# A two-layer fp32 mixer: a third plain feature tile, weight sums on VectorE, and layer 1's modulation moved into the down passes

## The chip, the cores and the metric

The kernel runs on one core of a Trainium2 chip. The metric is the device time of one execution in microseconds (us). Engines: PE (TensorE, matmuls), DVE (VectorE), ACT (ScalarE), POOL (GpSimd) and SP (SyncE), which issues all DMA transfers of this kernel.

## What is computed

Two layers of a transformer-like mixer on 512 latent tokens (stream X) and 256 context tokens (stream C), width 1024. The change touches the second half of a layer and the modulation vectors:

```python
for l in range(2):
    mod = silu(c) @ w_mod[l] + b_mod[l]          # 6 vectors of 1024; the same for c_ctx
    ...                                          # attention, local mixers -> mix
    x = layer_norm(ALPHA * x + g1 * (mix @ w_out), ln1g, ln1b)
    h = x * (1.0 + sc2) + sh2
    ffn = (silu(h @ w1) * (h @ w3)) @ w2         # 1024 -> 2816 -> 1024
    x = layer_norm(ALPHA * x + g2 * ffn, ln2g, ln2b)
```

Layer 0 does this for both streams (768 tokens), layer 1 for X alone (512).

## The kernel before

All matrix products are in fp32 made of three matmuls: `split` (L167 to L169) makes of an operand a high part (an ACT cast, L168) and a low part (a DVE subtraction, L169), and `mm3` (L172 to L174) adds low x high, high x low and high x high. Tokens lie in two halves of N columns, N = 384 in layer 0 and 256 in layer 1.

**The up phase** is `wout_ffn`. After the output projection and the first layer norm, `half` transposes a half's tokens and splits them into R[0] or R[1]. The 2816 hidden features are 22 tiles of 128. The first NCONV = 2 are plain: `conv` multiplies a tile's two weights (w1, w3) with one half, 48 matmuls, so 96 a tile. The other 20 are block tiles: seven products of 12 matmuls (`prod`, L1186) with sums of weights of N columns, 84 a tile. `up_forms` makes the sums: splits wa (of s1, for a11 and a12), wb (for s1 and a22), wc (for s2 and s4) and wd (for s3), with four 128x512 sums on POOL between them (L1073, L1074, L1077, L1078); wc hangs on all but one. The token side needs the differences T1 to T4 of the halves (L1177 to L1180), three kinds on DVE, one on POOL, and their splits. T3 takes over the buffers of R[1][0:4]. After the products, ACT copies partial sums (L1232 is one), DVE adds (L1194, L1218, L1233), and POOL multiplies by the gate (L1195, L1196). The output of a tile goes to DRAM (`yd`).

`spool` also writes the residual of the second layer norm to DRAM (`rd`): `residual` (L964) scales and shifts it first, two 128x1024 POOL operations (L966, L967) a token tile.

**The down phase** runs in passes: layer 0 in two passes of three token tiles, layer 1 in one of four. For each feature tile, `feat` loads its `yd` columns and its w2 weight, splits them, and `mm` multiplies; one feature tile is loaded ahead. At ft == 6 the residual comes back. `ffn_last` is the second layer norm (L1021 to L1046). After tiles X1 and X2 of pass 1, `hook` makes layer 1's first operands (groups of transposes, L360).

**Modulation of layer 1.** `mods` loads 512 KB pieces of w_mod, two for each of eight k groups, and multiplies them in small matmuls (L274), four a group. Three such generators are in `filler`; `fill(2)` takes two steps after each block tile of layer 0.

**What sets the order.** The order of the instructions on each engine is set by a scheduler that simulates the program; buffers come from pools in which a new tile waits for an old one's last reader (weights w 5, raw weights s 4, u 22, f 14 in the FFN, PSUM pairs pd 2, PSUM banks ps 4). Each engine, SP too, runs its own list in order.

Of the kernel before, what the change touches and what calls it, by code (L numbers as in the profile page):

```python
# [90 lines left out]
def hybrid_kernel(ctx: ExitStack, tc: tile.TileContext, out: bass.AP, g: dict):  # L91
# [996 lines left out]
    def wout_ffn(l, streams, final, hook=None):  # L1088
# [100 lines left out]
        def finish(ft, w, A, Bk, sa, su):  # L1189

            prod(A, w["s4"], B22, False, True)
            A_.activation(out=sa[:, 1], in_=A, func=AF.Silu)  # L1192
            prod(Bk, w["a22"], T4, False, True)
            V_.tensor_tensor(out=su[:, 0], in0=su[:, 0], in1=Bk, op=ALU.add)  # L1194
            G_.tensor_tensor(out=sa[:, 1], in0=sa[:, 1], in1=su[:, 1], op=ALU.mult)  # L1195
            G_.tensor_tensor(out=sa[:, 0], in0=sa[:, 0], in1=su[:, 0], op=ALU.mult)  # L1196

        def store(ft, sa):
            nc.sync.dma_start(out=yd[l][ft][:, :2 * N], in_=sa.rearrange("p a b -> p (a b)"))

        wn = up_forms(l, NCONV)
# [302 lines left out]
```

## Time and profile before

| | us |
|---|---|
| median of 3 runs (1714.37 to 1716.43) | 1716.4 |
| the profiled execution | 1715.44 |
| its span, first to last instruction | 1713.7 |
| PE busy in the span | 1590.8 (93%) |
| DVE busy | 1009.1 (59%) |
| ACT busy | 771.0 (45%) |
| POOL busy | 613.7 (36%) |

The mean granted clock of PE is 0.977 of full speed. Stages of the span, in us: layer 0's plain tiles end at 468, its block stage runs from 489 to some 850, its down passes to 1033; the boundary to layer 1 takes till 1080; layer 1's plain tiles run from 1314 to 1342, its block stage from 1350 to some 1580, its down pass from 1599 to 1703.

A busy share is a mean over stages with different limits; what an edit is worth is read in its own stage, from the idle time before an instruction (in brackets in a timeline row, with what ended it) and from what the releasing engine did meanwhile. In a timeline row the first number is the start, the second the time from the first start to the last end of xcount instructions; the step from one row's start to the next is what they cost.

### The profile page before, as it was taken

What the parts mean: (1) busy time and instruction counts of PE and PEld (TensorE: products, weight loads), DVE (VectorE), ACT (ScalarE), POOL (GpSimd) and SP (SyncE); (2) the same over time, 40 slices, a digit from 0 to 9 for tenths busy, and PEclk for the clock granted to TensorE, in tenths of its full rate; (3) what the DMA queues carried; (4) which work ended last, traced back from release to release, by engine and by line L of the source; (5) the groups of instructions that cost most, each with busy time, mean ns of one, the idle gap of its engine ahead of it and who ended that gap; (6) DMA issues with size and microseconds to landing.
All of it is one profiled execution on the core that took longest, in us unless ns stands there. A gap on an engine that the chain in (4) does not pass through costs nothing.

```text
span 1713.7 us, 24043 instructions
## 1 busy us (share of the span) xinstructions
PE 1590.8 (93%) x9105; PEld 1363.9 (80%) x9105; DVE 1009.1 (59%) x1361; ACT 771.0 (45%) x1381; POOL 613.7 (36%) x570
## 2 busy tenths in 40 slices
PE   6999889999859999999899998989999799997997
PEld 4757779887848777799888887879988798996886
DVE  1434777869853343354455437677769766567645
ACT  2422666865332232333443336478844444453311
POOL 0213012325635444455200105523325577772002
PEclk9999999999979999999999998999999899998999
DMA  9575113145335656634774625401164333456521
GB/s 336 169 230 169 58 38 118 56 147 185 108 119 179 198 168 182 187 127 122 228 228 130 207 70 168 125 25 38 38 221 144 109 116 114 123 161 193 174 86 50
DMA packets 180216, 241.81 MB, mean 141 GB/s; under 512 B 10842, under 2 KB 126924, under 8 KB 180100
## 3 DMA queue, kind: packets, MB, share of 16 engines
q1 hardware_dynamic: 180100, 240.28, 44.2%
q8 instruction: 71, 1.16, 0.3%
q14 instruction: 45, 0.37, 0.1%
HBM read 215.30 MB, written 24.94 MB: 140 GB/s over the span
## 4 chain that ended last, share of the span: by engine, by line
PE 69%; DVE 13%; DMA 5%; ACT 5%; issue 4%; POOL 3%; SPq 1%; DVEq 0%; POOLq 0%; ACTq 0%
PE pd L1186 18%; PE pd L172 9%; PE pd L173 9%; PE pd L174 9%; PE ps L274 4%; PE ps L172 4%; DVE u L169 4%; PE ps L174 4%; PE ps L173 4%; DVE w L169 3%; PE ps L731 3%; PE ps L1186 3%; PE ps L715 2%; ACT w L168 2%; DMA s<-in_w_ffn_dram 2%
## 5 line engine op out<-in xcount | busy, mean ns | idle before, releaser
L169 DVE TENSOR_TENSOR w<-s,w 128x1024 fp32r<-128x1024 f32 (+2 forms) x287 | 391.5, 1371 | 283.9 <-ACT w L168 282.0
L168 ACT CAST w<-s 128x1024 fp32r<-128x1024 f32 (+2 forms) x287 | 293.8, 1030 | 477.0 <-PE pd L1186 116.7
L1186 PE MATMUL pd<-u,w 128*128 128x256 f32 (+1 forms) x2040 | 320.6, 310 | 46.7 <-DVE w L169 30.3
L1186 PEld LDWEIGHTS pd<-u,w 128*128 128x128 f32 x2040 | 296.8, 191 | 76.6 <-DVE w L169 31.1
L172 PE MATMUL pd<-w,u 128*128 128x512 f32 (+5 forms) x728 | 276.2, 380 | 12.3 <-DVE u L169 6.4
L173 PE MATMUL pd<-w,u 128*128 128x512 f32 (+5 forms) x728 | 273.3, 376 | 1.9 <-DVE w L169 1.9
L174 PE MATMUL pd<-w,u 128*128 128x512 f32 (+5 forms) x728 | 271.6, 374 | 0.0
L172 PEld LDWEIGHTS pd<-w,u 128*128 128x128 f32 x728 | 139.2, 191 | 45.9 <-DVE u L169 8.7
L173 PEld LDWEIGHTS pd<-w,u 128*128 128x128 f32 x728 | 139.4, 191 | 27.9 <-issue 3.4
L169 POOL TENSOR_TENSOR u<-y,u 128x512 fp32r<-128x512 f32 (+1 forms) x60 | 78.8, 1321 | 226.4 <-ACT u L168 204.2
L174 PEld LDWEIGHTS pd<-w,u 128*128 128x128 f32 x728 | 139.2, 191 | 24.9 <-issue 1.7
L367 POOL TENSOR_SCALAR st<-st 128x1 f32<-128x1 f32 x30 | 9.0, 299 | 366.8 <-DVE st L1025 257.3
L168 ACT CAST u<-y 128x512 fp32r<-128x512 f32 (+2 forms) x178 | 94.6, 545 | 56.0 <-PE pd L1186 20.9
L1077 POOL TENSOR_TENSOR s<-s,s 128x512 f32<-128x512 f32 x40 | 67.0, 1676 | 135.9 <-DVE w L169 81.4
L169 DVE TENSOR_TENSOR u<-y,u 128x512 fp32r<-128x512 f32 (+2 forms) x118 | 74.5, 642 | 48.5 <-ACT u L168 47.7
L1195 POOL TENSOR_TENSOR f<-f,f 128x384 f32<-128x384 f32 (+1 forms) x40 | 60.8, 1521 | 70.9 <-ACT f L1192 70.9
L1073 POOL TENSOR_TENSOR y<-s,s 128x512 f32<-128x512 f32 x40 | 56.6, 1417 | 75.2 <-DMA s<-in_w_ffn_dram 68.8
L169 DVE TENSOR_TENSOR u<-ps,u 128x512 fp32r<-128x512 f32 (+2 forms) x106 | 67.1, 655 | 27.0 <-ACT u L168 25.8
L172 PE MATMUL ps<-w,u 128*128 128x512 f32 (+1 forms) x208 | 80.8, 395 | 1.1 <-ACT w L168 1.1
L173 PE MATMUL ps<-u,w 128*128 128x256 f32 (+2 forms) x224 | 76.0, 341 | 6.3 <-DVE u L169 6.3
L173 PE MATMUL ps<-w,u 128*128 128x512 f32 (+1 forms) x208 | 81.3, 392 | 0.0
L174 PE MATMUL ps<-w,u 128*128 128x512 f32 (+1 forms) x208 | 81.0, 391 | 0.0
(251 smaller groups left out, 2929.1 us busy)
## 6 DMA issues: line engine op xcount, KB each, us to landing
s<-in_w_ffn_dram SPq DMA_DIRECT2D x154, 512.0 KB
s<-in_w_mod_dram SPq DMA_DIRECT2D x80, 512.0 KB
s<-in_w_out_dram SPq DMA_DIRECT2D x50, 512.0 KB
u<-in_w_mod_dram SPq DMA_DIRECT2D x16, 512.0 KB
s<-in_w_in_dram SPq DMA_DIRECT2D x16, 512.0 KB
yd<-f SPq DMA_DIRECT2D x20, 384.0 KB
y<-yd SPq DMA_DIRECT2D x88, 64.0 KB
y<-yd SPq DMA_DIRECT2D x22, 256.0 KB
```

The lines of the kernel that those rows point to most:

```text
L168: A_.copy(out=hi, in_=src)
L169: (eng or V_).tensor_tensor(out=lo, in0=src, in1=f(hi), op=ALU.subtract)
L172: T_.matmul(ps, lhsT=ll, rhs=rh, start=start, stop=False)
L173: T_.matmul(ps, lhsT=lh, rhs=rl, start=False, stop=False)
L174: T_.matmul(ps, lhsT=lh, rhs=rh, start=False, stop=stop)
L274: T_.matmul(ps[32 * j:32 * j + 32, :n], lhsT=sst[:, k, :], rhs=ws[j // 2][:, (j % 2) * n:(j % 2 + 1) * n], start=(k == 0), stop=(k == KD - ...
L715: T_.transpose(pt[:, o:o + P], es[t2][:, k * P:(k + 1) * P], ident)
L731: T_.matmul(av[:, 0:256], lhsT=vt[k][:, h, :], rhs=pts[k // 2][:, a, (k % 2) * 256:(k % 2 + 1) * 256], start=(k == 0 and a == 1), stop=(k ...
L1073: G_.tensor_tensor(out=d, in0=s1[:, lo], in1=s3[:, lo], op=ALU.subtract)
L1077: G_.tensor_tensor(out=s1[:, lo], in0=s3[:, lo], in1=s1[:, lo], op=ALU.subtract)
L1186: T_.matmul(ps, lhsT=A[u][:, k], rhs=B[k][:, v], start=first and k == 0 and i == 0, stop=last and k == 3 and i == 2, skip_group_check=True)
L1195: G_.tensor_tensor(out=sa[:, 1], in0=sa[:, 1], in1=su[:, 1], op=ALU.mult)
```

## The change

1. NCONV is 3. The third plain tile's two halves stand after the second tile's second half, ahead of the first block product; 19 block tiles follow.
2. The four sums of `up_forms`, the two gate products of a block tile and the one kind of difference that POOL had go to DVE.
3. A block tile is a generator (`unit`) with five stops; the loop takes steps of the tile at hand and of the one before in turn. The first feature tile of the down phase is loaded ahead of the last tile's last products.
4. `spool` writes the plain residual; the scaling is done in the down phase at ft == 8, on POOL, as the residual comes back. Its scale vectors are loaded at the start of the down phase.
5. Layer 1's modulation goes from the block stage of layer 0 to its down passes, one step for each feature tile in pass 0 and six in pass 1; two of the three generators load ahead into `u` buffers.
6. `hook` makes the context's operands of layer 1 at ft == 6 of pass 1, and the first X ones after its second token tile. In pass 0's last tile the first feature tile of pass 1 is loaded ahead.

```diff
-    NCONV, NLAST = 2, 4
+    NCONV, NLAST = 3, 4
...
-            G_.tensor_tensor(out=d, in0=s1[:, lo], in1=s3[:, lo], op=ALU.subtract)
+            V_.tensor_tensor(out=d, in0=s1[:, lo], in1=s3[:, lo], op=ALU.subtract)
...
         def spool(st, t, n):
-            y = residual(n, bc)
-            nc.sync.dma_start(out=rd[l][st.jt + t], in_=y)
+            nc.sync.dma_start(out=rd[l][st.jt + t], in_=n)
...
-        for ft in range(NCONV):
+        for ft in range(2):
             conv(1, ft, *w13[ft])
+        for ft in range(2, NCONV):
+            w13.append((getw(("1", l, ft), 1), getw(("3", l, ft), 1)))
+            for hv in range(2):
+                conv(hv, ft, *w13[ft])
...
-            for e, o, i0, i1, t in ((V_, y11, y12, y11, T1), (G_, y12, y22, y12, T3), (V_, y22, y22, y11, T2),
-                                    (V_, y21, y21, y22, T4)):
-                e.tensor_tensor(out=o, in0=i0, in1=i1, op=ALU.subtract)
+            for o, i0, i1, t in ((y11, y12, y11, T1), (y12, y22, y12, T3), (y22, y22, y11, T2), (y21, y21, y22, T4)):
+                V_.tensor_tensor(out=o, in0=i0, in1=i1, op=ALU.subtract)
...
+            yield
+            prod(A, w["s4"], B22, False, True)
+            A_.activation(out=sa[:, 1], in_=A, func=AF.Silu)
+            V_.tensor_tensor(out=sa[:, 1], in0=sa[:, 1], in1=su[:, 1], op=ALU.mult)
+            yield
+            prod(Bk, w["a22"], T4, False, True)
+            V_.tensor_tensor(out=su[:, 0], in0=su[:, 0], in1=Bk, op=ALU.add)
+            V_.tensor_tensor(out=sa[:, 0], in0=sa[:, 0], in1=su[:, 0], op=ALU.mult)
+            yield
+            nc.sync.dma_start(out=yd[l][ft][:, :2 * N], in_=sa.rearrange("p a b -> p (a b)"))
...
+            cur = unit(ft, wn)
+            next(cur)
+            if ft + 1 < NF:
+                wn = up_forms(l, ft + 1)
+            if prev:
+                next(prev)
+            next(cur)
+            if prev:
+                next(prev)
+            next(cur)
+            if prev:
+                run(prev)
+            prev = cur
+        first = feat(0, 0)
+        run(prev)
...
+        if not final:
+            filler.extend([mods(1, (0, 1), 0, 512, run_ahead=True, src_=U), mods(1, (2, 3), 0, 512, run_ahead=True, src_=U),
+                           mods(1, (4, 5), 0, 512)])
...
-                if not final:
-                    fill(2)
-                if ft == 6:
+                if not final and (pi == 0 or ft < 6):
+                    fill(1)
+                if hook and pi and ft == 6:
+                    hook(res, 0)
+                if ft == 8:
                     for st, t in tiles:
                         y = FT()
                         nc.sync.dma_start(out=y, in_=rd[l][st.jt + t])
+                        G_.tensor_tensor(out=y, in0=y, in1=bc[0], op=ALU.mult)
+                        G_.tensor_tensor(out=y, in0=y, in1=bc[1], op=ALU.add)
                         ya.append(y)
...
-        if l == 0:
-            filler += [mods(1, (0, 1), 0, 512), mods(1, (2, 3), 0, 512), mods(1, (4, 5), 0, 512)]
```

**PE in layer 0, from the plain tiles to the block tiles** (L172 to L174 are a plain tile's matmuls, L1186 and in the change L1187 a block product's; `u_3989` and the three behind it are an operand's four quarters). Before:

```order
L173 MATMUL ps_4540<-u_4404,w_811_4283 128x384
L174 MATMUL ps_4540<-u_4404,w_811_4283 128x384
L1186 MATMUL ps_4677<-u_3989,w_863_4659 128x384 x3
L1186 MATMUL ps_4677<-u_3990,w_863_4659 128x384 x3
L1186 MATMUL ps_4677<-u_3991,w_863_4659 128x384 x3
L1186 MATMUL ps_4677<-u_3992,w_863_4659 128x384 x3
L1186 MATMUL pd_4676<-u_4597,w_866_4670 128x384 x3
```

With the change:

```order
L173 MATMUL ps_4634<-u_4392,w_842_4573 128x384
L174 MATMUL ps_4634<-u_4392,w_842_4573 128x384
L1187 MATMUL pd_4770<-u_3979,w_865_4753 128x384 x3
L1187 MATMUL pd_4770<-u_3980,w_865_4753 128x384 x3
L1187 MATMUL pd_4770<-u_3981,w_865_4753 128x384 x3
L1187 MATMUL pd_4770<-u_3982,w_865_4753 128x384 x3
L1187 MATMUL ps_4771<-u_3983,w_865_4753 128x384 x3
L1187 MATMUL ps_4771<-u_3984,w_865_4753 128x384 x3
L1187 MATMUL ps_4771<-u_3985,w_865_4753 128x384 x3
L1187 MATMUL ps_4771<-u_3986,w_865_4753 128x384 x3
L1187 MATMUL pd_4770<-u_4691,w_868_4764 128x384 x3
```

Before, the last plain matmul is followed by the product a12 (into `ps`), which needs no difference, and then by s2, which needs T2's splits (`u_4597`). Now the 96 matmuls of a third plain tile (`w_842` is one of its weights) stand between the second tile and the first block product; then come a11 and a12, and then s2, with `w_868`.

**DVE in the middle of layer 1's block stage.** Before, one tile's share of the list:

```order
L1218 TENSOR_TENSOR f_12816<-f_12816,ps_12815 128x256
L169 TENSOR_TENSOR f_12892<-y_12881,f_12892 128x512
L1233 TENSOR_TENSOR f_12697<-f_12697,pd_12694 128x256
L169 TENSOR_TENSOR w_2077_12884<-s_2063_12756,w_2077_12884 128x1024
L1233 TENSOR_TENSOR f_12817<-f_12817,pd_12814 128x256
L1194 TENSOR_TENSOR f_12697<-f_12697,pd_12694 128x256
L169 TENSOR_TENSOR w_2078_12889<-s_2062_12754,w_2078_12889 128x1024
L169 TENSOR_TENSOR w_2086_12998<-s_2073_12874,w_2086_12998 128x1024
L169 TENSOR_TENSOR w_2088_13004<-s_2074_12876,w_2088_13004 128x1024
L1218 TENSOR_TENSOR f_12936<-f_12936,ps_12935 128x256
L1194 TENSOR_TENSOR f_12817<-f_12817,pd_12814 128x256
```

With the change:

```order
L1077 TENSOR_TENSOR s_2048_12698<-s_2049_12700,s_2048_12698 128x512
L169 TENSOR_TENSOR w_2063_12828<-s_2049_12700,w_2063_12828 128x1024
L1220 TENSOR_TENSOR f_12789<-f_12789,ps_12788 128x256
L1236 TENSOR_TENSOR f_12670<-f_12670,pd_12667 128x256
L169 TENSOR_TENSOR f_12836<-y_12825,f_12836 128x512
L1078 TENSOR_TENSOR s_2048_12698<-s_2048_12698 128x512
L1073 TENSOR_TENSOR y_12945<-s_2059_12818,s_2060_12820 128x512
L1237 TENSOR_TENSOR f_12669<-f_12669,f_12670 128x256
L1074 TENSOR_TENSOR s_2060_12820<-s_2060_12820 128x512
L169 TENSOR_TENSOR w_2064_12833<-s_2048_12698,w_2064_12833 128x1024
L169 TENSOR_TENSOR w_2072_12942<-s_2059_12818,w_2072_12942 128x1024
L1220 TENSOR_TENSOR f_12909<-f_12909,ps_12908 128x256
```

The sums L1073 to L1078 and the products L1233 and L1237 of the change now stand among the splits (L169) and the additions (before L1194, L1218 and L1233, in the change L1220, L1229 and L1236). On PE the order of the block products in the middle of this stage is the same in both kernels: s3 and s1 of one tile, s2 of the next, a12 of the one after, s4 of the first, and so on.

**SP in layer 0, pass 0** (`yd_4` is the up phase's output of feature tile 4; L1267 and L1203 are `feat`'s loads). Before, from feature tile 5 on:

```order
L1267 DMA y_7448<-yd_5_118 128x128 x3
L1267 DMA y_7478<-yd_6_119 128x128 x3
L1267 DMA y_7508<-yd_7_120 128x128 x3
L1267 DMA y_7544<-yd_8_121 128x128
L186 DMA s_1162_7392<-in_w_ffn_dram 128x1024
L1267 DMA y_7544<-yd_8_121 128x128 x2
L1267 DMA y_7574<-yd_9_122 128x128 x3
L186 DMA s_1166_7422<-in_w_ffn_dram 128x1024
L1267 DMA y_7604<-yd_10_123 128x128 x3
```

With the change, from feature tile 4 on:

```order
L1239 DMA yd_19_132<-f_6667 128x768
L260 DMA u_7098<-in_w_mod_dram 128x1024
L1203 DMA y_7179<-yd_4_117 128x128
L260 DMA u_7100<-in_w_mod_dram 128x1024
L1203 DMA y_7179<-yd_4_117 128x128
L260 DMA u_7137<-in_w_mod_dram 128x1024
L260 DMA u_7139<-in_w_mod_dram 128x1024
L1203 DMA y_7179<-yd_4_117 128x128
L1203 DMA y_7217<-yd_5_118 128x128 x3
L1203 DMA y_7255<-yd_6_119 128x128
L186 DMA s_1101_7145<-in_w_ffn_dram 128x1024
L1203 DMA y_7255<-yd_6_119 128x128 x2
```

Loads of w_mod (L260) now stand among the loads of `feat`; before, none does.

## Rows read from the trace of the kernel before

**Rows 1.** Table by stage: busy us of PE, PEld, DVE, ACT, POOL, PEclk, DMA, GB/s.

```profile
858.00:940.00 82.00, 82.00 (x354) 66.21 (x353) 42.43 (x57) 30.71 (x42) 0.91 (x3) 1.00 0.58 180
...
1033.00:1080.00 47.00, 38.63 (x199) 34.35 (x198) 33.47 (x53) 27.56 (x60) 20.68 (x25) 0.85 0.57 177
```

**Rows 2.** Timeline of PE, block tile of layer 0: start, us, matmul, count.

```profile
761.48 7.51 PE L1186 MATMUL pd<-u,w 128*128 128x384 f32 x42
...
776.17 1.04 PE L1186 MATMUL pd<-u,w 128*128 128x384 f32 x5
```

**Rows 3.** Timeline of PE, layer 0, plain to block tiles; idle before in brackets.

```profile
468.49 2.26 PE L1186 MATMUL ps<-u,w 128*128 128x384 f32 x12
488.99 2.29 PE L1186 MATMUL pd<-u,w 128*128 128x384 f32 x6 [18.25 <-DVE w L169]
...
493.00 2.79 PE L1186 MATMUL pd<-u,w 128*128 128x384 f32 x12
```

**Rows 4.** Timeline of DVE, the same stretch.

```profile
452.31 10.61 DVE L169 TENSOR_TENSOR u<-f,u 128x384 fp32r<-128x384 f32 x6 [2.25 <-ACT u L168]
...
476.75 0.54 DVE L169 TENSOR_TENSOR u<-f,u 128x384 fp32r<-128x384 f32 x1
```

**Rows 5.** Timeline of POOL, the same stretch.

```profile
452.28 4.90 POOL L1179 TENSOR_TENSOR f<-f 128x384 f32<-128x384 f32 x4
457.15 2.70 POOL L967 TENSOR_TENSOR f<-f,f 128x1024 f32<-128x1024 f32 x1
459.81 2.70 POOL L966 TENSOR_TENSOR f<-f,f 128x1024 f32<-128x1024 f32 x1
462.47 3.18 POOL L1073 TENSOR_TENSOR y<-s,s 128x512 f32<-128x512 f32 x2
```

**Rows 6.** Timeline of DVE, layer 1, plain to block tiles.

```profile
1333.76 6.73 DVE L169 TENSOR_TENSOR u<-f,u 128x256 fp32r<-128x256 f32 x7
...
1343.77 2.09 DVE L169 TENSOR_TENSOR u<-f,u 128x256 fp32r<-128x256 f32 x6
```

**Rows 7.** Timeline of PE, layer 1, first block sum product.

```profile
1350.05 2.29 PE L1186 MATMUL pd<-u,w 128*128 128x256 f32 x9 [6.36 <-DVE w L169]
```

**Rows 8.** Timeline of PE, two block tiles of layer 1.

```profile
1453.50 7.54 PE L1186 MATMUL pd<-u,w 128*128 128x256 f32 x60
...
1465.13 1.58 PE L1186 MATMUL pd<-u,f 128*128 128x256 f32 x12
1466.54 1.59 PE L1186 MATMUL pd<-u,w 128*128 128x256 f32 x12
1469.27 1.67 PE L1186 MATMUL pd<-u,w 128*128 128x256 f32 x12 [1.14 <-ACT f L1232]
...
1475.59 0.64 PE L1186 MATMUL pd<-u,w 128*128 128x256 f32 x4
```

**Rows 9.** Timeline of PE, L274 alone and two halves together.

```profile
65.33 1.06 PE L274 MATMUL ps<-s,sst 128*32 128x512 f32 x8
...
499.92 1.05 PE L274 MATMUL ps<-s,sst 128*32 128x512 f32 x4
500.90 2.39 PE L1186 MATMUL ps<-u,w 128*128 128x384 f32 x12
```

**Rows 10.** Timeline of DVE, end of layer 1's block stage.

```profile
1544.77 0.68 DVE L169 TENSOR_TENSOR u<-y,u 128x512 fp32r<-128x512 f32 x1
...
1546.64 1.22 DVE L169 TENSOR_TENSOR w<-s,w 128x1024 fp32r<-128x1024 f32 x1
...
1559.29 1.23 DVE L189 TENSOR_TENSOR s<-s,f 128x1024 f32<-128x1024 f32 x1 [2.14 <-DMA s<-in_w_ffn_dram]
```

**Rows 11.** Table by stage, densest transfers.

```profile
33.00:43.00 10.00, 9.88 (x79) 7.68 (x72) 3.36 (x6) 5.52 (x9) 0.00 (x0) 1.00 1.06 389
```

**Rows 12.** Groups by line, DVE, 1350 to 1540: busy us, mean ns, idle before.

```profile
L169 DVE TENSOR_TENSOR w<-s,w 128x1024 fp32r<-128x1024 f32 x52 | 73.9, 1436 | 64.5 <-ACT w L168 64.5
```

**Rows 13.** Timeline of PE, layer 1, block stage to down pass.

```profile
1561.71 2.93 PE L1186 MATMUL pd<-u,w 128*128 128x256 f32 x12 [5.72 <-DVE w L169]
```

More of the change, by code (lines that the diff above doesn't have):

```diff
@@ L1157, in wout_ffn @@
         w13 = []
-        for ft in range(NCONV):
+        for ft in range(2):
             w13.append((getw(("1", l, ft), 1), getw(("3", l, ft), 1)))
-        for ft in range(NCONV):
+        for ft in range(2):
             conv(0, ft, *w13[ft])
@@ L1166, in wout_ffn @@
             spool(C, 1, ns[1])
-        for ft in range(NCONV):
+        for ft in range(2):
             conv(1, ft, *w13[ft])
+        for ft in range(2, NCONV):
+            w13.append((getw(("1", l, ft), 1), getw(("3", l, ft), 1)))
+            for hv in range(2):
+                conv(hv, ft, *w13[ft])
         if both:
@@ L1187, in prod, with feat, unit @@
                               stop=last and k == 3 and i == 2, skip_group_check=True)
[L1189 to L1201, printed above, removed]
-        prev, stored = None, None
-        gb = {}
-        for ft in range(NCONV, NF):
-            if ft == NF - 4:
-                gb = {st.s: gates(l, 1, st.s, FT) for st in streams}
-                if final:
-                    gbox.append(gb[0])
-            w = wn
+        passes = [[(X, t) for t in range(4)]] if final else [[(C, 0), (C, 1), (X, 0)], [(X, 1), (X, 2), (X, 3)]]
+        def feat(pi, ft):
+            tiles = passes[pi]
+            n = len(tiles) * P
+            y = Y(n)
+            i = 0
+            while i < len(tiles):
+                st, t = tiles[i]
+                c, m = col[(st.s, t)], 1
+                while i + m < len(tiles) and col[(tiles[i + m][0].s, tiles[i + m][1])] == c + m * P:
+                    m += 1
+                nc.sync.dma_start(out=y[:, i * P:(i + m) * P], in_=yd[l][ft][:, c:c + m * P])
+                i += m
+            w2 = getw(("2", l, pi, ft), 1)
+            d = U(F32R, 2 * n).rearrange("p (a b) -> p a b", a=2)
+            split(d[:, 0], d[:, 1], y)
+            return d, w2
+        def unit(ft, w):
             pd = PD()
@@ new lines, in wout_ffn @@
+        prev, old = None, None
+        wn = up_forms(l, NCONV)
+        gb = {}
+        for ft in range(NCONV, NF):
+            if ft == NF - 4:
+                gb = {st.s: gates(l, 1, st.s, FT) for st in streams}
+                if final:
+                    gbox.append(gb[0])
+            cur = unit(ft, wn)
[11 more added lines that the diff above has]
+            prev = cur
@@ L1248, in wout_ffn @@
         for pi, tiles in enumerate(passes):
-            n = len(tiles) * P
             accs, ya = [], []
-            kinds = "sdds" if final else ("dds" if pi == 0 else "sdd")
-            for c in kinds:
+            for c in "sdds" if final else ("dds" if pi == 0 else "sdd"):
                 if c == "d":
@@ L1284, in wout_ffn @@
                 if ft + 1 < NF - NLAST:
[L1285 removed]
+                    nx = feat(pi, ft + 1)
                 for i in range(len(tiles)):
                     mm(i, [ft], [d])
[L1288 to L1290 removed]
+                if not final and (pi == 0 or ft < 6):
[3 more added lines that the diff above has]
+                if ft == 8:
                     for st, t in tiles:
@@ L1385, in extras, with hook @@
                 next(p)
-    def hook(res, st, t):
-        if (st.s, t) not in HOOK:
-            return
-        grp = HOOK[(st.s, t)]
+    def hook(res, i):
+        grp = HOOK[i]
         if not AB:
-            fill(99)
+            while len(filler) > 2:
+                fill(1)
             for s_ in (C, X):
```

62 lines of the change are left out of this document (17 added, 45 removed).

## The prediction

> **What bounds the kernel now.** I read three views in this order: the table by stage, then TensorE's (PE's) timeline in each stage that has holes, then the queues of the engines that feed it.
>
> The table by stage splits the kernel in two. In the down passes of layer 0 (858 to 940 us) PE is busy all the time at a granted clock of 1.00: there only fewer or denser matmuls help. Between the stages it is not: at the boundary of the layers, from 1033 to 1080, PE is busy 38.63 of 47 us at 0.85 [rows 1]. A block tile of layer 0 takes 776.17 − 761.48 = 14.69 us for 84 matmuls without a hole [rows 2], 0.175 us each.
>
> In two places the holes have the same cause. After the second plain tile of layer 0, PE issues one product at 468.49, then waits 18.25 us; the next twelve matmuls need 493.00 − 488.99 = 4.01 us where the settled rate gives 2.10 [rows 3]. The hole is the time in which VectorE (DVE) still makes operands: six 128x384 splits take 10.61 us from 452.31, against 0.54 for one at 476.75 [rows 4]. In the same ten microseconds GpSimd (POOL) runs 4.90 + 2.70 + 2.70 us of its own six operations [rows 5]: one POOL operation for each DVE one. When POOL falls silent, the DVE operation is three times as fast. In layer 1 it is the same, seven 128x256 splits in 6.73 us against six in 2.09 later [rows 6], and PE then waits 6.36 us [rows 7].
>
> The Trainium skill ("SBUF — State Buffer", SBUF: two separate sides) calls this an exclusive lock on a port pair that a two-input DVE operation and a POOL operation share, the loser fully blocked; the trace agrees, 1.77 us against 0.54.
>
> In the block stage of layer 1 a pair of tiles takes 1475.59 − 1453.50 = 22.09 us with a hole of 1.14 in it [rows 8]; 168 matmuls at 1.42 us a dozen (1466.54 − 1465.13 is 1.41) are 19.9, so 2.2 us a pair are lost.
>
> **The change, part by part** (a plus is a gain, in us).
>
> *Third plain tile, layer 0: +15.* It costs 96 matmuls for the 84 of the block tile it replaces: 12 × 0.175 = 2.1. Its own 16.8 us fill the hole: 18.25, and 1.9 of slow matmuls behind it [rows 3]. The operands will be there earlier, since POOL does nothing in this stretch now: the residual (L966, L967), the sums and one kind of difference are gone from it, and some 35 operations at 0.47 to 0.55 need 17 to 19 us, till about 465, where the splits of the third tile's weights follow. A new wait comes: as the order of the change shows, the lo part of `wc`, which s2 needs, stands on DVE behind L1220, which waits for a12; L1220 and that split are 0.5 + 1.2 [rows 4, 10], so about 1.9 of hole stay. 18.25 + 1.9 − 2.1 − 1.9 = 16.2; I take 15, for weights that land late. Bounds 8 and 18.
>
> *Third plain tile, layer 1: +11.* The DVE list from 1321.66 to 1347 shrinks by some 13 us at the 0.35 of one undisturbed split [rows 6], so the plain tiles of this half run at PE's rate from about 1322: three tiles at 11.36 and two products of 1.42 end near 1348, and s2 starts at 1349 to 1350, as before [rows 7]. By then PE has done 11.36 + 1.42 more, of which 1.42 is extra work. Bounds 7 and 13.
>
> *Modulation matmuls (L274), layer 0: +12.* The two instructions of half a k group (four records) stand alone in 44 of 46 places of the block stage; one such place costs 500.90 − 499.92 = 0.98 (the row itself 1.05). Where the halves stand together, eight records take 1.06, the same as four [rows 9]. In the change's order they stand in 32 places, one of six and one of nine instructions: 14 × 0.98 = 13.7, less some 2 for the long ones. Bounds 9 and 14.
>
> *Their loads, now in the down passes: −6.* Two loads of 512 KB a k group are 1.05 MB; at the 389 GB/s of the densest stretch [rows 11] that is 2.70 us. A feature tile of pass 0 takes some 4.1 us, of which the DMA engines are busy 0.58 [rows 1], 2.4 us. 2.4 + 2.7 = 5.1, against 4.1 + 0.98 of PE. It just fits, so I book a quarter of a microsecond for each of 24 groups. Bounds 0 and −15.
>
> *Operations moved from POOL to DVE: 0 in layer 0.* A 128x512 one takes 0.68 on DVE, a split 1.22 [rows 10], a small one of layer 1 0.35 [rows 6]; for a block tile of layer 1 that is 3 × 1.15 + 5 × 0.6 + 5 × 0.35 = 8.2 us (the steps between starts are some 0.08 shorter than the rows), in layer 0 8.8. In layer 0 the tile lasts 14.69 us, which covers it.
>
> *The same in the block stage of layer 1: +9.* s2 waits for the last link of a chain (two sums, a split, two sums, a split). DVE's 128x1024 split averages 1.436 there [rows 12] instead of 1.22, and four POOL sums of 1.4 to 1.6 (a pair took 3.18 at 462.47 [rows 5]) become four of 0.6: the chain gets about 4 us shorter, and a tile lacks 1.1. But the order of the products on PE is the same before and after, so the interleaving itself gives nothing, and DVE is filled to 8.2 of 9.93 us with four waits for PE or ScalarE (ACT) in each tile. I take 9 of 19 × 1.1 = 21. Bounds 0 and 18.
>
> The Trainium skill ("Perfetto Trace Analysis", Optimizing Scalar/DVE Operations) says that moving work between GpSimd and DVE might not help, as they share a read port, and that a saturated DVE is one to unload. By the first half this term would be near 0, which is rival (a).
>
> *Boundary between the layers: +6.* The context's last rows and their transposes leave 1033 to 1080 for pass 1. PE idles there 8.4 us [rows 1]; the remaining X rows still have to come. Bounds 0 and 9.
>
> *Up to down, layer 1: +3.* The largest hole, 5.72 at 1561.71 [rows 13], follows a DVE wait of 2.14 for a w2 load ahead of the split [rows 10]. The change loads the first down tile before the last products; the queue past that stays. Bounds −3 and 9.
>
> *Residual scaling in the down passes: 0.* Twelve POOL operations in layer 0 and eight in layer 1, of some 2.7 [rows 5], on an engine that is busy 0.91 of 82 us [rows 1]. Each can hold one DVE split back by its own length; the next tile's operands are made one tile (4.1 us) ahead, which is the cover, and its loss would cost 2.7 a time. Bounds −3 and 0.
>
> Sum: 15 + 11 + 12 − 6 + 9 + 6 + 3 = 50. The profiled execution took 1715.4 us (span 1713.7 and 1.7 around it), one below the median, so **1716.4 − 50 = 1666.4**.
>
> **The rivals.**
> (a) *DVE becomes the bound in layer 1.* For it: 82% fill and one queue in order. Against: most of its waits are for products that PE has finished by then. The tile stays at 11 us, and the terms of the block stage and of up to down go: 50 − 12 = 38, 1678.
> (b) *The holes move instead of closing.* The third tile's weights need splits too, and T3's splits wait for the tile's own last reads, so PE may meet a late operand behind it. Against: that is 2.4 us of DVE. Then only the 4 us of lower losses stay of 26: 50 − 22 = 28, 1688.
> (c) *The loads pace layer 0's down passes (slower).* All transfers go through SP, in order; the order rows show four modulation loads among the three pieces of feature 4, each of them into a U tile that must be free first, and features 5 and 6 stand behind. If nothing of a load is hidden, 24 × 2.70 = 64.8 us are lost where I booked 6: 50 − 58.8 = −9, 1725. It turns from gain to loss at 56 / 24 = 2.3 us of PE wait a group. Against: the DMA engines are half idle there, and tiles are loaded ahead.
>
> The Trainium skill ("DMA: Bandwidth & Descriptors", Queues, rings and completion order) has each DMA engine take descriptors in ring order, which speaks for (c); no run here shows it.
>
> (d) *It does not do what it says:* nothing but the order changes and the scheduler's holes stay, within 0.2%, 1715. Against: the order rows show the third tile in the hole.
>
> **How the numbers follow.** Chances: my forecast 0.65, (a) 0.15, (b) 0.10, (c) 0.07, (d) 0.03. All favourable bounds of the larger terms with the rest as booked (18 + 13 + 14 + 0 + 18 + 6 + 3) give 72, 1644; the forecast with a quiet loss in each gives (a) and (b). The range that leaves out (c), (d) and the rarest tails is 1644 to 1692. A measurement here tells changes over 0.2% (3.4 us) apart: faster 0.90, same 0.03, slower 0.07.
>
> **What would show it.** In the changed profile: no hole over 3 us at the first block product of either layer; 128x384 splits at 0.47 to 0.55 throughout; a pair of block tiles in layer 1 at 20 to 21 us; L274 in about 32 groups; PE free of holes in pass 0. Wrong would be: holes marked by a load of yd, w2 or w_mod in the down passes of layer 0 (c); a layer 1 period of 22 us with DVE busy over 80% (a); a hole of over 5 us behind the third tile (b).

## The result, and the profile after

The change takes 1669.9 us (median of 4 runs, 1668.66 to 1673.28); the ratio to the kernel before is 0.9739 (95% interval 0.9721 to 0.9756), 45 us faster. The forecast was 1666.4. The profiled execution took 1668.66 us, its span is 1666.9.

First the three places with holes. PE's timeline from the plain to the block tiles of layer 0 (start, us, matmul, count, idle before and what ended it), which answers to [rows 3]:

```profile
481.76 2.25 PE L1187 MATMUL pd<-u,w 128*128 128x384 f32 x12
483.85 2.27 PE L1187 MATMUL ps<-u,w 128*128 128x384 f32 x12
487.91 1.31 PE L1187 MATMUL pd<-u,w 128*128 128x384 f32 x6 [1.78 <-DVE w L169]
```

DVE and POOL in the same stretch, for [rows 4, 5]; POOL is idle from 437 to 709 us:

```profile
457.88 1.49 DVE L169 TENSOR_TENSOR u<-f,u 128x384 fp32r<-128x384 f32 x3
...
461.63 1.22 DVE L169 TENSOR_TENSOR w<-s,w 128x1024 fp32r<-128x1024 f32 x1
...
486.64 3.49 DVE L169 TENSOR_TENSOR w<-s,w 128x1024 fp32r<-128x1024 f32 x3
```

```profile
709.71 0.53 POOL L240 MEMSET y<- 128x512 f32 x1 [272.27 <-DVE f L169]
```

Three splits take 1.49 us together, where one took 1.77, and the hole of 18.25 is one of 1.78, at the place forecast for it: s2 waits behind L1220. In layer 1 the hole of 6.36 [rows 7] is 2.88:

```profile
1317.60 5.49 PE L1187 MATMUL pd<-u,w 128*128 128x256 f32 x24 [2.88 <-DVE w L169]
```

The block stage of layer 1, PE's timeline over one pair, and the DVE group for [rows 8, 12]:

```profile
1411.34 1.57 PE L1187 MATMUL pd<-u,w 128*128 128x256 f32 x12
1413.26 1.68 PE L1187 MATMUL pd<-u,w 128*128 128x256 f32 x12 [0.34 <-DVE w L169]
...
1432.11 2.07 PE L1187 MATMUL pd<-u,w 128*128 128x256 f32 x16
```

```profile
L169 DVE TENSOR_TENSOR w<-s,w 128x1024 fp32r<-128x1024 f32 x47 | 56.9, 1222 | 15.1 <-ACT w L168 15.1
```

From s1 to the s1 of the next pair 1432.11 − 1411.34 = 20.77 us, against 22.1; over twelve tiles the mean step is 20.84, against 22.05 before. The hole is 0.34, and the split is back at 1.222. DVE is busy for 132.99 of 164 us there (table by stage):

```profile
1332.00:1496.00 164.00, 161.56 (x1327) 157.79 (x1326) 132.99 (x206) 83.50 (x143) 0.00 (x0) 1.00 0.45 136
```

Two things went the other way. Between pass 0 and pass 1 of layer 0 there are holes that were not there before; PE's timeline, the queue of SP, and the table by stage (columns as in [rows 1]):

```profile
929.03 0.44 PE L360 MATMUL ps<-ident,f 128*128 128x128 f32 x2 [1.20 <-ACT y L362]
932.72 0.69 PE L360 MATMUL ps<-ident,f 128*128 128x128 f32 x2 [3.25 <-ACT y L362]
934.43 0.69 PE L360 MATMUL ps<-ident,f 128*128 128x128 f32 x2 [1.02 <-ACT y L362]
...
942.25 0.80 PE L172 MATMUL ps<-w,u 128*128 128x512 f32 x1 [4.65 <-DVE u L169]
```

```profile
919.32 15.89 SPq L186 DMA_DIRECT2D s<-in_w_ffn_dram  x9
935.27 9.65 SPq L1203 DMA_DIRECT2D y<-yd  x14
```

```profile
785.00:860.00 75.00, 75.00 (x351) 51.01 (x350) 37.72 (x42) 24.22 (x31) 18.70 (x8) 1.00 0.91 317
...
920.00:943.00 23.00, 11.57 (x45) 6.22 (x44) 9.77 (x14) 12.39 (x21) 0.00 (x0) 0.74 0.74 240
```

Nine w2 loads stand in SP's queue for 15.89 us, and the first `yd` load of pass 1 comes behind them at 935.27; meanwhile PE is busy for 11.57 of 23 us and its clock is granted at 0.74 in the mean, between its two levels (2.4 and 1.2 GHz). In pass 0 itself (785 to 860) PE is busy throughout at a DMA share of 0.91. And the holes from the block stage to the down pass of layer 1 stayed:

```profile
1499.06 3.10 PE L1187 MATMUL pd<-u,w 128*128 128x256 f32 x24 [2.65 <-DVE w L169]
...
1512.33 2.93 PE L1187 MATMUL pd<-u,w 128*128 128x256 f32 x12 [5.92 <-DVE w L169]
```

Where the time went, from starts in both traces (the first score matmul of layer 1's attention, L731, marks the end of the boundary):

| us | before | after | gained so far |
|---|---|---|---|
| last block product of layer 0 | 855.5 | 781.1 | 74.4 |
| first L731 of layer 1 | 1155.6 | 1126.9 | 28.6 |
| last transpose (L1114) of layer 1 | 1320.7 | 1288.1 | 32.6 |
| last block product of layer 1 | 1595.2 | 1542.9 | 52.4 |
| last matmul | 1703.9 | 1657.0 | 46.9 |

Of the 74.4 us, the down passes give 45.8 back. PE's time added up by line in both traces (from a start to the next one, less the idle time) shows on what. The L274 matmuls, 46 us of the block stage before, take 34.4 in the change, and 27.7 of these stand behind the last block product: that much is a move. Most of the other 18 are new losses between that product and L731: PE is idle for 22.4 us instead of 13.3, the matmuls of the down passes (L172 to L174) take 280.9 instead of 275.4, and the L360 transposes 2.5 more. What follows is about which part earned what.

### The profile page after: what moved, and what is told of

Read it like the earlier page. It is cut to its first block, busy times and chain, and to the rows that moved or that the text cites. A ratio compares the mean times of both kernels' runs of the same rounds, so it can differ in the third digit from the quotient of the medians.

```text
span 1666.9 us, 23834 instructions
## 1 busy us (share of the span) xinstructions
PE 1572.3 (94%) x9129; PEld 1358.9 (82%) x9129; DVE 1045.8 (63%) x1591; ACT 769.3 (46%) x1371; POOL 260.6 (16%) x322
## 4 chain that ended last, share of the span: by engine, by line
PE 81%; DVE 8%; DMA 4%; ACT 4%; issue 2%; SPq 0%; POOL 0%; POOLq 0%; DVEq 0%; ACTq 0%
PE pd L1187 21%; PE pd L172 10%; PE pd L173 10%; PE pd L174 10%; PE ps L172 5%; PE ps L173 5%; PE ps L174 5%; PE ps L1187 4%; PE ps L274 3%; PE ps L731 3%; PE ps L715 2%; DVE w L169 2%; DVE u L169 2%; DMA u<-in_w_mod_dram 1%; DMA s<-in_w_ffn_dram 1%
## 5 line engine op out<-in xcount | busy, mean ns | idle before, releaser
L168 ACT CAST w<-s 128x1024 fp32r<-128x1024 f32 (+3 forms) x285 | 292.7, 1031 | 473.0 <-PE pd L1187 141.2
L169 DVE TENSOR_TENSOR w<-s,w 128x1024 fp32r<-128x1024 f32 (+3 forms) x285 | 352.5, 1244 | 195.8 <-ACT w L168 195.7
L1187 PE MATMUL pd<-u,w 128*128 128x256 f32 (+1 forms) x1938 | 295.4, 308 | 19.0 <-DVE w L169 14.3
L1187 PEld LDWEIGHTS pd<-u,w 128*128 128x128 f32 x1938 | 282.7, 191 | 25.2 <-DVE w L169 15.8
L172 PE MATMUL pd<-w,u 128*128 128x512 f32 (+5 forms) x728 | 277.9, 383 | 8.3 <-DVE u L169 3.6
L174 PE MATMUL pd<-w,u 128*128 128x512 f32 (+5 forms) x728 | 272.9, 376 | 0.0
L172 PEld LDWEIGHTS pd<-w,u 128*128 128x128 f32 x728 | 140.3, 193 | 54.6 <-issue 16.3
L174 PEld LDWEIGHTS pd<-w,u 128*128 128x128 f32 x728 | 140.2, 193 | 27.2 <-issue 4.2
L169 DVE TENSOR_TENSOR u<-y,u 128x512 fp32r<-128x512 f32 (+2 forms) x118 | 77.7, 679 | 63.0 <-ACT u L168 61.8
L169 POOL TENSOR_TENSOR u<-y,u 128x512 fp32r<-128x512 f32 (+1 forms) x60 | 78.9, 1323 | 225.5 <-ACT u L168 203.2
L172 PE MATMUL ps<-u,w 128*128 128x256 f32 (+2 forms) x288 | 92.1, 328 | 1.8 <-DVE modT L300 1.1
L174 PE MATMUL ps<-u,w 128*128 128x256 f32 (+2 forms) x288 | 93.5, 327 | 0.0
L173 PE MATMUL ps<-u,w 128*128 128x256 f32 (+2 forms) x288 | 93.3, 326 | 0.1
L172 PE MATMUL ps<-w,u 128*128 128x512 f32 (+1 forms) x208 | 81.2, 398 | 5.6 <-DVE u L169 4.7
L169 DVE TENSOR_TENSOR u<-ps,u 128x512 fp32r<-128x512 f32 (+2 forms) x106 | 66.7, 654 | 28.8 <-ACT u L168 27.8
L174 PE MATMUL ps<-w,u 128*128 128x512 f32 (+1 forms) x208 | 81.4, 393 | 0.0
L1304 POOL TENSOR_TENSOR f<-f,f 128x1024 f32<-128x1024 f32 x10 | 25.8, 2598 | 333.5 <-DMA f<-rd 254.4
L1187 PE MATMUL ps<-u,w 128*128 128x384 f32 (+1 forms) x456 | 75.3, 313 | 0.0
```

What stands on the lines that cost most here:

```text
L168: A_.copy(out=hi, in_=src)
L169: (eng or V_).tensor_tensor(out=lo, in0=src, in1=f(hi), op=ALU.subtract)
L172: T_.matmul(ps, lhsT=ll, rhs=rh, start=start, stop=False)
L173: T_.matmul(ps, lhsT=lh, rhs=rl, start=False, stop=False)
L174: T_.matmul(ps, lhsT=lh, rhs=rh, start=False, stop=stop)
L1187: T_.matmul(ps, lhsT=A[u][:, k], rhs=B[k][:, v], start=first and k == 0 and i == 0, stop=last and k == 3 and i == 2, skip_group_check=True)
```

## The experiments

All ratios are to the kernel before on the same chip; the differences in us are those of the ratios times 1714.

| run | us | ratio (95% interval) | against the change |
|---|---|---|---|
| the change | 1669.9 | 0.9739 (0.9721 to 0.9756) | |
| two plain tiles | 1672.5 | 0.9757 (0.9742 to 0.9773) | +3 |
| residual back | 1685.6 | 0.9831 (0.9804 to 0.9859) | +16 |
| both of these | 1681.1 | 0.9810 (0.9795 to 0.9825) | +12 |
| sums on POOL | 1677.0 | 0.9785 (0.9770 to 0.9800) | +8 |
| modulation back in the block stage | 1691.3 | 0.9865 (0.9844 to 0.9885) | +22 |
| third set in u buffers | 1661.3 | 0.9692 (0.9676 to 0.9709) | −8 |
| late hook | 1661.0 | 0.9694 (0.9678 to 0.9710) | −8 |
| third set in u, residual on DVE | 1650.6 | 0.9629 (0.9612 to 0.9646) | −19 |
| the same with the late hook | 1641.2 | 0.9571 (0.9550 to 0.9591) | −29 |
| before, with the third tile | 1697.3 | 0.9906 (0.9891 to 0.9921) | |
| before, with the residual moved | 1706.2 | 0.9954 (0.9940 to 0.9969) | |
| before, with POOL's sums, gate products and difference on DVE | 1699.7 | 0.9918 (0.9903 to 0.9933) | |

### Which part closed the holes

**Two plain tiles.**

```diff
-    NCONV, NLAST = 3, 4
+    NCONV, NLAST = 2, 4
```

> The change with two plain tiles instead of three, all else kept. Theory A (the third tile fills the hole in front of s2): the hole comes back in both layers, over 8 us in layer 0 and over 4 in layer 1, and the time is 1680 to 1695. Theory B (the hole was made by POOL slowing DVE's splits, and would be nearly gone without the third tile): in the changed kernel the last T2 split ends at 465.8 us and the sums can start at once, so the hole in layer 0 is 3 to 6 us, 12 matmuls less are done in each layer, and the time is within 4 us of the changed kernel, 1666 to 1674.

Measured 0.9757: the time is in theory B's range, and the intervals of the two kernels overlap. PE's timeline of this run, layer 0 and layer 1:

```profile
474.81 2.29 PE L1187 MATMUL pd<-u,w 128*128 128x384 f32 x6 [7.07 <-DVE w L169]
```

```profile
1312.35 5.49 PE L1187 MATMUL pd<-u,w 128*128 128x256 f32 x24 [8.46 <-DVE w L169]
```

The holes come back, somewhat larger than theory B had them, but layer 0's is 7.07 us, not 18.25, and each is paid for in part with twelve matmuls fewer. Layer 1's, 8.46, is longer than before; the plain tiles ahead of it no longer wait themselves (one waits 3.99 us at 1336.70 in the kernel before, in this run none over 0.32). With POOL silent the third tile earns about 3 us, which is not clear of the noise.

**Residual back ahead of the up phase**, with three plain tiles and with two.

```diff
         def spool(st, t, n):
-            nc.sync.dma_start(out=rd[l][st.jt + t], in_=n)
+            y = residual(n, bc)
+            nc.sync.dma_start(out=rd[l][st.jt + t], in_=y)
...
-                        G_.tensor_tensor(out=y, in0=y, in1=bc[0], op=ALU.mult)
-                        G_.tensor_tensor(out=y, in0=y, in1=bc[1], op=ALU.add)
```

> The change with the residual's scaling back on POOL ahead of the up phase. Theory A (each POOL operation holds one DVE split back): the 128x384 splits of layer 0 and the 128x256 ones of layer 1 take 1.0 to 1.8 us again while L966 and L967 run, DVE's list ends some 10 us later; the third tile covers most, so 3 to 10 us slower over both layers, 1673 to 1680. Theory B (the splits were slow for another reason): splits stay at 0.47 to 0.55, time within 3 us of the changed kernel.

> Two plain tiles and the residual's scaling back ahead of the up phase: the fourth corner with the changed kernel, two plain tiles alone, and the residual alone. Theory A (the third tile is worth more where POOL holds DVE back, since there is a hole to fill): at least 8 us slower than the residual alone, 1692 to 1702. Theory B (the two add up, each its own): the residual alone plus 2 to 4, 1686 to 1691.

Measured +16 and +12. DVE, POOL and PE of the first run:

```profile
452.41 2.70 DVE L169 TENSOR_TENSOR u<-f,u 128x384 fp32r<-128x384 f32 x1
455.20 2.55 DVE L1182 TENSOR_TENSOR f<-f 128x384 f32<-128x384 f32 x1
457.68 2.70 DVE L169 TENSOR_TENSOR u<-f,u 128x384 fp32r<-128x384 f32 x1
...
460.95 0.55 DVE L169 TENSOR_TENSOR u<-f,u 128x384 fp32r<-128x384 f32 x1
```

```profile
452.15 2.54 POOL L967 TENSOR_TENSOR f<-f,f 128x1024 f32<-128x1024 f32 x1
454.66 2.68 POOL L966 TENSOR_TENSOR f<-f,f 128x1024 f32<-128x1024 f32 x1
457.42 2.55 POOL L967 TENSOR_TENSOR f<-f,f 128x1024 f32<-128x1024 f32 x1
```

```profile
455.16 0.69 PE L173 MATMUL ps<-u,w 128*128 128x384 f32 x1 [4.11 <-DVE u L169]
```

Three DVE operations in a row end 0.4 us after three POOL operations in a row and take as long as these; the next one, with POOL done, takes 0.55. Theory A holds, and the price is above its 3 to 10 us: the operands held back are those of the plain tiles of half 1, so PE waits (4.11 at 455.16) ahead of the third tile, which cannot cover that. The two-tile run, 1681.1, lies below both of its ranges: it is not slower than the three-tile one, so the guess that the third tile is worth more here fell. The intervals overlap, and which of the two is faster stays open.

**Each part alone on the kernel before.** To the kernel before, in turn:

```diff
-    NCONV, NLAST = 2, 4
+    NCONV, NLAST = 3, 4
...
+        for ft in range(2, NCONV):
+            w13.append((getw(("1", l, ft), 1), getw(("3", l, ft), 1)))
+            for hv in range(2):
+                conv(hv, ft, *w13[ft])
```

```diff
-            y = residual(n, bc)
-            nc.sync.dma_start(out=rd[l][st.jt + t], in_=y)
+            nc.sync.dma_start(out=rd[l][st.jt + t], in_=n)
...
                         nc.sync.dma_start(out=y, in_=rd[l][st.jt + t])
+                        G_.tensor_tensor(out=y, in0=y, in1=bc[0], op=ALU.mult)
+                        G_.tensor_tensor(out=y, in0=y, in1=bc[1], op=ALU.add)
```

```diff
-            G_.tensor_tensor(out=d, in0=s1[:, lo], in1=s3[:, lo], op=ALU.subtract)
+            V_.tensor_tensor(out=d, in0=s1[:, lo], in1=s3[:, lo], op=ALU.subtract)
...
-            for e, o, i0, i1, t in ((V_, y11, y12, y11, T1), (G_, y12, y22, y12, T3), (V_, y22, y22, y11, T2),
+            for e, o, i0, i1, t in ((V_, y11, y12, y11, T1), (V_, y12, y22, y12, T3), (V_, y22, y22, y11, T2),
...
-            G_.tensor_tensor(out=sa[:, 1], in0=sa[:, 1], in1=su[:, 1], op=ALU.mult)
+            V_.tensor_tensor(out=sa[:, 1], in0=sa[:, 1], in1=su[:, 1], op=ALU.mult)
```

> The kernel before with a third plain tile alone. Theory A (as forecast, its matmuls fill the holes in front of s2: 15 and 11 us): 1686 to 1698. Theory B (the hole is POOL's hold on DVE; a third tile brings two more weights to split and 12 more matmuls in each layer, and what it fills it gives back): 1704 to 1716.

> The kernel before with the residual's scaling moved to the down passes alone, still on POOL. Theory A (those POOL operations hold DVE's splits in the plain stage): the hole in front of s2 in layer 0 shrinks from 18 to under 10 us, 10 to 18 us faster, 1696 to 1704. Theory B (the sums and the one kind of difference on POOL hold DVE just as well): within 5 us of the kernel before, 1709 to 1718.

> The kernel before with the sums, the gate products and the one kind of difference on DVE alone. Theory A (both the block stage of layer 1, 1.2 us a pair, and the plain stages gain): the pair falls from 22.05 to 20.8, 11 to 12 us, and the holes give 5 to 10 more, 1692 to 1699. Theory B (only the pair): 1702 to 1705. If DVE were the bound (rival a): the pair stays at 22 and nothing is gained, 1710 to 1718.

Measured 16, 8 and 14 us faster: in theory A's range, between the two theories, and just above theory A's range (1699.7 against 1692 to 1699). The first s2 of layer 0 in the three, PE's timeline:

```profile
495.02 1.31 PE L1190 MATMUL pd<-u,w 128*128 128x384 f32 x6 [1.78 <-DVE w L169]
```

```profile
477.09 2.29 PE L1184 MATMUL pd<-u,w 128*128 128x384 f32 x6 [10.74 <-DVE w L169]
```

```profile
485.51 2.29 PE L1186 MATMUL pd<-u,w 128*128 128x384 f32 x6 [6.81 <-DVE w L169]
```

Each closes much of the same hole of 18.25: the third tile by filling it (theory A there), the other two by making it shorter. That is why the third tile is worth 16 us put in first and about 3 put in last, and why single gains do not add up. The residual moved alone gains 10.6 us to the end of the block stage (its last product starts at 844.9 instead of 855.5) and gives some back at once, because its POOL operations now stand where pass 0's operands are split. DVE and POOL of that run:

```profile
843.17 3.40 DVE L169 TENSOR_TENSOR w<-s,w 128x1024 fp32r<-128x1024 f32 x1
846.49 4.94 DVE L169 TENSOR_TENSOR u<-y,u 128x384 fp32r<-128x384 f32 x4
```

```profile
842.79 2.69 POOL L1293 TENSOR_TENSOR f<-f,f 128x1024 f32<-128x1024 f32 x1
845.44 3.37 POOL L1294 TENSOR_TENSOR f<-f,f 128x1024 f32<-128x1024 f32 x1
```

The 128x1024 split takes 3.40 instead of 1.22.

**Sums on POOL.**

```diff
-            V_.tensor_tensor(out=d, in0=s1[:, lo], in1=s3[:, lo], op=ALU.subtract)
+            G_.tensor_tensor(out=d, in0=s1[:, lo], in1=s3[:, lo], op=ALU.subtract)
...
```

> The change with the four weight sums of a block tile back on POOL. Theory A (the chain of sums and splits sets the period of layer 1's block tiles, and POOL makes it longer): a pair of block tiles in layer 1 goes back to 21.5 to 22.1 us, 10 to 20 us slower, 1680 to 1690. Theory B (the gate products and the lost lock are what helped there): the pair stays under 20.6 us, within 4 us of the changed kernel.

Measured +8, just under theory A's range and outside B's. The hole ahead of s2 is back:

```profile
1416.07 1.65 PE L1187 MATMUL pd<-u,w 128*128 128x256 f32 x12 [1.19 <-DVE w L169]
```

The mean step of a pair over twelve tiles is 21.65 us, or 21.47 if they begin one tile later: of the 1.21 us that the change takes off a pair, the sums are 0.6 to 0.8, the rest of the moved work what is left. POOL to DVE alone on the kernel before gives 20.85, the whole 1.2, without the interleaving of `unit`; rival (a), DVE as the bound, is excluded by both.

### The modulation and the down passes

**Modulation back in the block stage**, from s buffers, two steps a tile.

```diff
             prev = cur
+            fill(2)
...
-        if not final:
-            filler.extend([mods(1, (0, 1), 0, 512, run_ahead=True, src_=U), mods(1, (2, 3), 0, 512, run_ahead=True, src_=U),
-                           mods(1, (4, 5), 0, 512)])
...
+        if l == 0:
+            filler += [mods(1, (0, 1), 0, 512), mods(1, (2, 3), 0, 512), mods(1, (4, 5), 0, 512)]
```

> The change with layer 1's modulation back in layer 0's block stage, two steps a tile, from s buffers. Theory A (moving it was worth the 6 us forecast, 12 for denser matmuls less 6 for the loads): 1673 to 1679. Theory B (the loads cost the down passes as much as the denser matmuls gave): within 4 us of the changed kernel, 1666 to 1673, with L274 in 40 or more places of the block stage, and pass 0 and the step to pass 1 without the holes of 1.2 to 4.65 us.

Measured +22: neither theory. PE's groups of block products in that run and in the change (count, ns, first and last start):

```profile
L1187 PE MATMUL pd<-f,w x342: 331/338/522, 487.7 to 836.6; 128*128 128x384 f32 x171
```

```profile
L1187 PE MATMUL pd<-f,w x342: 332/337/445, 489.1 to 781.1; 128*128 128x384 f32 x171
```

```profile
826.82 4.21 PE L1187 MATMUL pd<-u,w 128*128 128x384 f32 x12 [3.35 <-DVE f L1229]
```

From the first such product to the last it is 836.6 − 487.7 = 348.9 us against 292.0, so 56.9 more. PE's time by line shows what they are. L274 takes 45.2 us, in 45 places, against 6.7, since 36 of the change's 192 also stand ahead of that last product: 38.5. The same 1565 block products take 287.9 against 274.9: 13.0. Idle time is 4.8 against 1.1: 3.7, most of it the hole of 3.35 at the stage's end. The rest is 1.7. Of the 13.0 some 8 to 9 lie beside the L274 places:

```profile
497.67 2.35 PE L1187 MATMUL ps<-u,w 128*128 128x384 f32 x12
499.96 1.05 PE L274 MATMUL ps<-s,sst 128*32 128x512 f32 x4
```

Twelve products between two such places take 499.96 − 497.67 = 2.29 us, where the settled rate gives 2.10. So a place costs 0.2 more than its own 0.98. The others lie at the two ends of the stage; 3.3 of them come behind 820, where the clock is granted at 0.79 (820 to 830).

From there to the first L731 it is 1150.0 − 836.6 = 313.4 against 1126.9 − 781.1 = 345.8: in the down passes the same modulation, loads and all, costs 32.4. The L274 matmuls there are 27.7 of it; the down passes' own matmuls take 280.9 against 278.5, and PE idles 22.4 against 21.6. So the loads can have cost some 3 us at most. And the holes ahead of pass 1 are in this run too, though no modulation load is near them; SP and PE:

```profile
945.08 16.71 SPq L186 DMA_DIRECT2D s<-in_w_ffn_dram  x5
```

```profile
967.21 0.79 PE L172 MATMUL ps<-w,u 128*128 128x512 f32 x1 [4.19 <-DVE u L169]
```

**Third set in u buffers, loaded ahead.**

```diff
-                           mods(1, (4, 5), 0, 512)])
+                           mods(1, (4, 5), 0, 512, run_ahead=True, src_=U)])
```

> The change with the third set of modulation loads in u buffers and ahead, as the first two. Theory A (in the changed kernel these loads share four s buffers with the w2 loads, SP stands still for a free one, and the yd loads of pass 1 stand behind nine w2 loads till 935 us): the holes of 1.2, 3.25, 1.0 and 4.65 us before pass 1 shrink by more than half, 5 to 12 us faster, 1658 to 1665. Theory B (the rate of the DMA engines paces pass 0): the wait only moves, within 3 us of the changed kernel.

Measured −8, in theory A's range. SP and PE of this run:

```profile
903.95 18.95 SPq L186 DMA_DIRECT2D s<-in_w_ffn_dram  x6
926.42 13.70 SPq L1203 DMA_DIRECT2D y<-yd  x26
```

```profile
922.22 0.44 PE L360 MATMUL ps<-ident,f 128*128 128x128 f32 x2 [0.66 <-ACT y L362]
...
931.03 0.80 PE L172 MATMUL ps<-w,u 128*128 128x512 f32 x1 [0.97 <-DVE u L169]
```

`yd` loads start at 926.42 instead of 935.27, the wait ahead of pass 1's first matmul falls from 4.65 to 0.97, and all holes there together from 11.4 us to 5.6; what is left are mostly holes of 0.66 between the context's transposes. But theory A's cause is not shown. SP's queue stands here too, for 18.95 us with six w2 loads in it, as it does with the modulation back in the block stage. In all three kernels most of SP's wait is for DVE's splits of w2, which free the s buffers (25.3 us in ten waits from 895 to 965 in the change). And PE comes to the first of these holes at 921.56 instead of 927.83, so 6.3 us are won before any of them. Of the 8.9 us from the last block product to L731, 4.9 are the L274 matmuls, which take 22.8 instead of 27.7: all of them now stand in 27 places instead of 32. Idle time gives 2.7 (19.7 for 22.4), the down passes' matmuls 2.2 (278.7 for 280.9), and the L360 transposes take back 0.9. The larger part is thus the denser order of the small matmuls, which neither theory named.

**Late hook**, after token tiles X1 and X2 of pass 1.

```diff
-                if hook and pi and ft == 6:
-                    hook(res, 0)
...
-                if hook and pi and i == 1:
-                    hook(res, 1)
+                if hook and pi and i < 2:
+                    hook(res, i)
```

> The change with hook after token tiles X1 and X2 of pass 1, as before, all else kept. Theory A (making the context's operands early empties the boundary): the boundary loses 4 to 9 us more and the time is 1672 to 1678. Theory B (the early transposes only stand in front of pass 1, where the holes of 1.2, 3.25 and 1.0 us are before L360): those holes go, the boundary gets them, within 3 us of the changed kernel.

Measured −8: both theories fell. The early transposes cost more than they take from the boundary: the scheduler put them ahead of pass 1's first matmuls, where each pair of them waits for ACT to clear the one before. Without them PE idles 14.0 us instead of 22.4 from the last block product of layer 0 to L731.

**Residual on DVE** (with the third set in u), one token tile a feature tile; then with the late hook too.

```diff
-                if ft == 8:
-                    for st, t in tiles:
...
-                        G_.tensor_tensor(out=y, in0=y, in1=bc[0], op=ALU.mult)
-                        G_.tensor_tensor(out=y, in0=y, in1=bc[1], op=ALU.add)
+                if 8 <= ft < 8 + len(tiles):
+                    st, t = tiles[ft - 8]
...
+                    V_.tensor_tensor(out=y, in0=y, in1=bc[0], op=ALU.mult)
+                    V_.tensor_tensor(out=y, in0=y, in1=bc[1], op=ALU.add)
```

> The third set in u buffers, and the residual's scaling in the down passes on DVE, one token tile a feature tile from ft 8 on. Theory A (the eight POOL operations of layer 1's down pass hold DVE's splits back and make the hole of 6.76 us at 1549, and those of pass 0 and 1 cost some more): that hole falls under 2 us, 5 to 10 us faster than the third set alone, 1651 to 1657. Theory B (that hole waits for w2 loads, not for DVE): within 3 us of it, 1658 to 1664.

> The third set in u buffers, the residual's scaling on DVE, and hook after token tiles X1 and X2 as before. Theory A (early transposes hurt only because pass 1's first features were late behind the s buffers, and that is gone already): within 3 us of the same kernel with the early hook, 1648 to 1654. Theory B (each costs on its own): 4 to 9 us faster, 1642 to 1647.

Measured 0.9629 against 0.9692 with the third set alone (11 us), and 0.9571 with the late hook (10 more): theory A, then B, each time up to 1 us beyond the range. Layer 1's down pass with the scaling on POOL (PE, DVE, POOL of the third set alone), and DVE with the scaling on DVE:

```profile
1549.31 0.80 PE L173 MATMUL ps<-w,u 128*128 128x512 f32 x1 [6.76 <-DVE w L169]
```

```profile
1529.84 0.41 DVE L1236 TENSOR_TENSOR f<-f,pd 128x256 f32<-128x256 f32 x1
1530.28 2.18 DVE L1237 TENSOR_TENSOR f<-f,f 128x256 f32<-128x256 f32 x1
...
1535.74 11.24 DVE L169 TENSOR_TENSOR u<-y,u 128x512 fp32r<-128x512 f32 x4
```

```profile
1529.59 2.59 POOL L1305 TENSOR_TENSOR f<-f,f 128x1024 f32<-128x1024 f32 x1
1532.13 5.94 POOL L1304 TENSOR_TENSOR f<-f,f 128x1024 f32<-128x1024 f32 x2
1538.03 8.40 POOL L1305 TENSOR_TENSOR f<-f,f 128x1024 f32<-128x1024 f32 x3
```

```profile
1536.25 2.50 DVE L169 TENSOR_TENSOR u<-y,u 128x512 fp32r<-128x512 f32 x4
```

Four 128x512 splits take 11.24 us beside POOL and 2.50 without; the hole of 6.76 that waits for them is gone. In the change itself PE's holes there are smaller, 2.19 and 1.43. The last run, 1641.2 us, beats both kernels.

## Why the prediction was right, and where its sum was not

The time came out 3.5 us above the forecast and within the range. The terms behind it were right in kind for the plain and block stages; for the modulation, the hook and the residual they were off by up to 16 us, in both directions, and the errors cancelled. That the total came so near is in good part luck.

- *Third plain tile, +15 and +11.* The holes closed as forecast, to 1.78 and 2.88. But "its own 16.8 us fill the hole" credits the wrong edit: taken out of the change the tile costs about 3 us, while the residual back costs 16. The text had named POOL's hold on DVE as the hole's cause and then priced a filling for it. Both are true from one side: put in first, the tile gives 16, and even that is less than the 26 booked for the two layers.
- *Modulation matmuls, +12, and their loads, −6.* Net +22 instead of +6. The matmuls themselves came out as forecast, 46 places to 32 and 45.9 us to 34.4. The sum left out what a place costs the products beside it, some 0.2 us, 8 to 9 in the block stage, and the ends of that stage, where holes and a slow clock, about as much again, are gone with the modulation. The loads cost at most some 3 instead of 6: in pass 0 PE is busy throughout, so rival (c) did not happen.
- *Boundary, +6.* Wrong in sign. The step "the context's last rows and their transposes leave 1033 to 1080" assumed that PE would have other work while they run; ahead of pass 1 it had none, and the early hook costs 8 us.
- *Between pass 0 and pass 1* the sum had no term. The holes there are 11.4 us. The `yd` loads of pass 1 stand behind w2 loads, with the third set in s buffers, in u buffers, or elsewhere altogether. Taking the third set out of the s buffers gave 8 us, of which more than half comes from L274 matmuls that stand together, not from the holes.
- *Residual scaling, 0.* The text priced a lost cover at 2.7 a time; it is lost in layer 1, where eight POOL operations stand at the start of the down pass. Moving them to DVE gave, with pass 0 and 1, 11 us.
- *Block stage of layer 1, +9.* 1.21 us a pair over nine and a half pairs are 11.5. The chain of sums was the larger part of it (0.6 to 0.8 of 1.21), as forecast, and the order of the products on PE, the same in both, no part.
- *Up to down, layer 1, +3.* Nothing: 5.92 for 5.72 [rows 13].

The rule of the Trainium skill that moving work between GpSimd and DVE might not help ("Perfetto Trace Analysis", Optimizing Scalar/DVE Operations) did not decide here: the move alone is 14 us faster, with DVE busy in that run for 128.81 of 158 us of layer 1's block stage (1372 to 1530).

What stays open: why the third tile with the residual back is no faster than two tiles; why the block stage ends with holes when the modulation is in it; what paces the w2 splits for which SP's queue stands ahead of pass 1; and what `unit` and the loads ahead earn outside layer 1's block stage, since no run takes them out.

## What to carry to other kernels

When two engines hold each other back, look first at moving the shorter list away, and price the operations in the place where they arrive: a POOL operation of 2.6 us that was moved stopped a DVE split there just as well. Edits that close the same hole must be tried both alone and last; the single gains do not add. Price small matmuls between large ones with what they do to their neighbours: here a place cost 0.2 us beside its own 0.98. And where one queue issues all loads, look which of them wait for a buffer: nine w2 loads stood for 15.89 us and kept back the small ones that the next pass needed. Then take the suspected cause away and look again: here the queue stood without it as well.

## What the runs showed of the hardware

In the rows above, a DVE operation with two SBUF inputs that meets a POOL operation waits for its end: 2.55 to 2.70 us for one of 0.55, beside POOL operations of 2.54 to 2.68, one for one. A DVE operation with one input in PSUM does not: L1236 took its 0.41 at 1529.84, inside a POOL operation from 1529.59 to 1532.18, while L1237 right behind it, with two SBUF inputs, took 2.18. In the kernel before, 30 such 128x256 operations with a PSUM input began beside a POOL operation, and none took over 0.42. The Trainium skill ("SBUF — State Buffer", SBUF: two separate sides) states the first, an exclusive lock for the whole instruction against two SBUF inputs. The runs agree with it.
